# A hybrid convolution and RG-LRU block: recurrent channels laid out so that three of four heads fill the rows of one tile, and two low parts and a sum formed by accumulating DMA

## The chip, the cores and the metric

The kernel runs on one core of one Trainium2 chip. The metric is the device time of one execution in microseconds (us). Engines are named as the profile names them: PE (matrix multiply), PEld (its weight loads), DVE (vector), ACT (scalar, activations), POOL (GpSimd, used here to issue DMAs that add to their destination), SP (issues plain DMAs).

## The reference

One layer, sequence 1024, width 1024, everything in float32:

```python
h = rms_norm(x, g_mix)
z = h @ w_in + b_in                       # 1024 -> 7168
va, ga, xb, gb, sa, sb = split(z)         # 1024, 1024, 1536, 1536, 1024, 1024
u = causal_depthwise_conv(va * sigmoid(ga), conv_a_w, conv_a_b)      # width 31
y_a = silu(layer_norm(u)) @ w_a_out
v = causal_depthwise_conv(xb, conv_b_w, conv_b_b)                    # width 4
# rg_lru: 16 heads of 96 channels, block-diagonal 96x96 matrices
r = sigmoid(heads(v) @ w_rg_a + b_rg_a);  i = sigmoid(heads(v) @ w_rg_x + b_rg_x)
a = exp(-8 * r * softplus(-lam));         b = sqrt(1 - a*a) * i * v
h_t = a_t * h_{t-1} + b_t
y_b = (h * gelu(gb)) @ w_b_out
x = x + (sigmoid(sa) * y_a + sigmoid(sb) * y_b) @ w_o
x = x + square(relu(rms_norm(x, g_mlp) @ w_1)) @ w_2
out = rms_norm(x, g_final)
```

## The kernel before

Every float32 product is made of three products of rounded parts: a high part `h` and a low part `l = x - h` of each operand, and `hh + hl + lh` on PE. Low parts come either from `split` (ACT rounds, DVE subtracts) or from `split_dma`: ACT writes `l = -x` rounded, a POOL DMA adds `x` to it, ACT writes `h`. Channels stand on the 128 partitions, positions along the free axis (1024).

The change lies in the first projection stage and in what hangs on it. That stage is a hand-written order (`manual_schedule`: each engine executes its instructions in the order in which the Python code issues them). It goes through 28 column chunks of `w_in` of 128 columns each, in the order of the list `CH`. Chunks 0 to 2 are made earlier; **slot s** is the pass of the loop `for s in range(3, NC1)` in which PE makes chunk s (48 matmuls of 128x512; 24 pairs of operands, two halves) while the other engines work on the chunk before it. `CH` is XB0, VA0, GA0, XB1, XB2, VA1, GA1, XB3 to XB5, VA2, GA2, XB6 to XB8, VA3, GA3, XB9 to XB11, and then VA4, GA4 to VA7, GA7 in pairs. So the twelve `xb` tiles (12 x 128 = 1536 channels) come in four groups of three, and XB3, XB4, XB5 are taken out of the accumulator in slots 8, 9, 10.

What is done with an `xb` tile t: `xb_out` (ACT writes `xb` and a first tap of `v`, then three more taps of the width-4 convolution on DVE, called `rest` below), `xb_parts` (ACT writes the high half `vth`, DVE subtracts for the low half `vtl`). In the layout before, head n has channels 96n to 96n+95, which lie across tile borders: four heads fill three tiles. `head_load` therefore gathers a head's rows out of one or two tiles by SP DMAs (table `PIECES`). `head_mm(n, gi)` makes gate gi (0: r, 1: i) of a head, six matmuls into the one accumulator pair of tag `ps2`, which has a single buffer, so that PE cannot start a head product before ACT has read the one before. `head_gate` is that read: a sigmoid on ACT, and then SP DMAs scatter the 96 rows to one or two gate tiles `gate[gi, t]`.

Head n has slot `HS0[n]`: `head_mm(n, 0)` is at the end of that slot, `head_gate(n, 0)`, `head_mm(n, 1)` (after 36 of the 48 matmuls) and `head_gate(n, 1)` are in the next. In ACT's order within a slot stand `head_gate(before, 0)`, `xb_out`, the split of the next chunk's weights (`w_parts`: two copies), the square roots of `scan_root`, `xb_parts`, `head_gate(before, 1)`, the split of the next head's weights (`rgh`; DVE makes `rgl`), and the exponentials of `scan_exp`. Four heads are a group; `EXP` is the slot after the fourth head's: there ACT makes six exponentials and tanh, and `scan_in` (DVE: gate i times v) is issued for the group's first two tiles, and one slot later for its third. `scan_tile` is the recurrence itself. Slots of ten and more microseconds of DVE time that are not taken are filled by `fill` with taps of the width-31 convolution `conv` (one tap: one DVE instruction of 128x~511), whose count per slot a planner fixes at build time from assumed costs (`clk`); the order that comes of it is then fixed on the chip.

At the end of each of the eight convolutions its result `acc` goes to DRAM by SP, and DVE adds it to `ysum`, the sum that the layer norm later takes its mean from (128x1024).

## Time and profile before

| | |
|---|---|
| median of 3 runs | 1534.11 us (1533.87 to 1534.23) |
| the profiled execution | 1534.4 us, span 1532.6 us |
| granted PE clock | 0.999 |
| PE / PEld busy | 1522.9 us (99%) / 1252.9 us (82%) |
| DVE / ACT / POOL busy | 1217.2 us (79%) / 911.8 us (59%) / 172.6 us (11%) |
| instructions | 19039 |

The slots 3 to 27 lie between about 43 and 361 us of the span. A timeline row has the start in us, the duration in us, engine, line, operation, tiles and shape, a count, and in brackets the idle time before it with what ended it. A row of the chain has start, duration and what. Line numbers are those of the kernel before.

### The profile page before, as it was taken

Reading aid. Unit: us, or ns where it says so; the run is one execution under the profiler, and the core shown is the slowest. Engines: PE = TensorE matmul, PEld = TensorE weight load, DVE = VectorE, ACT = ScalarE, POOL = GpSimd, SP = SyncE. Lnnn points to the kernel's source line nnn. Section 1 sums busy time; section 2 is a strip of 40 time slices with the busy share of each in tenths; the row PEclk is TensorE's granted clock in tenths of the full one; section 3 lists DMA queues with packets and bytes.
Section 4 is the critical chain, followed back from the end, with each engine's and each line's share of the span. In section 5 each row is a group of like instructions: output and inputs, shape, how many; then the busy total and the mean of one; then the engine's idle time right before and its main releaser. Section 6 shows DMA issues by size and latency. Waiting matters only on the chain.

```text
span 1532.6 us, 19039 instructions
## 1 busy us (share of the span) xinstructions
PE 1522.9 (99%) x6734; PEld 1252.9 (82%) x6734; DVE 1217.2 (79%) x1647; ACT 911.8 (59%) x1273; POOL 172.6 (11%) x205
## 2 busy tenths in 40 slices
PE   9999999999999999999999999999999999999998
PEld 7878887888888888888888888888888888888886
DVE  6899999979999998778769879755555386777777
ACT  6648576657667666735475877554444455545475
POOL 0000000002222222000022322000000000101010
PEclk9999999999999999999999999999999999999999
DMA  8776978899998888963779898333333974776465
GB/s 349 198 188 159 250 185 215 223 274 224 241 255 209 198 193 229 311 230 117 265 199 301 197 194 210 138 117 112 112 112 110 304 266 124 177 209 170 109 123 153
DMA packets 132577, 304.68 MB, mean 199 GB/s; under 512 B 13264, under 2 KB 35280, under 8 KB 132480
## 3 DMA queue, kind: packets, MB, share of 16 engines
q1 hardware_dynamic: 104048, 234.79, 46.6%
q0 software_dynamic: 28288, 68.40, 24.4%
q8 instruction: 53, 0.87, 0.2%
q14 instruction: 44, 0.36, 0.1%
q10 hardware_dynamic: 144, 0.26, 0.0%
HBM read 149.79 MB, written 60.82 MB: 137 GB/s over the span
## 4 chain that ended last, share of the span: by engine, by line
PE 91%; issue 4%; DMA 2%; POOL 1%; DVE 1%; ACT 0%; SPq 0%; POOLq 0%; DVEq 0%
PE z L726 18%; PE d1b L1952 2%; PE d2b L1952 2%; PE d0b L1952 2%; PE d3b L1952 2%; PE d0e L1952 1%; PE d3e L1952 1%; PE d3a L1952 1%; PE d2e L1952 1%; PE d2a L1952 1%; PE d1e L1952 1%; PE d1a L1952 1%; PE z L258 1%; PE rg L534 1%; PE rg L536 1%
## 5 line engine op out<-in xcount | busy, mean ns | idle before, releaser
L726 PE MATMUL z<-xh,win_h 128*128 128x512 f32 x400 | 124.9, 390 | 0.0
L726 PE MATMUL z<-xl,win_h 128*128 128x512 f32 x400 | 124.5, 389 | 0.0
L726 PE MATMUL z<-xh,win_l 128*128 128x512 f32 x400 | 98.2, 391 | 0.0
L726 PEld LDWEIGHTS z<-xh,win_l 128*128 128x128 f32 x400 | 75.1, 188 | 16.9
L726 PEld LDWEIGHTS z<-xh,win_h 128*128 128x128 f32 x400 | 75.0, 188 | 16.7 <-ACT win_h L67 0.7
L637 DVE SCALAR_TENSOR_TENSOR y<-u,vec,y 128x511 f32<-128x511 f32 (+14 forms) x120 | 88.6, 739 | 0.0
L726 PEld LDWEIGHTS z<-xl,win_h 128*128 128x128 f32 x400 | 75.1, 188 | 15.8
L542 ACT ACTIVATE g<-rg,vec 96x1024 f32<-96x1024 f32 x32 | 35.6, 1113 | 85.4 <-issue 43.2
L637 DVE SCALAR_TENSOR_TENSOR yt<-u,vec,yt 128x511 f32<-128x511 f32 (+6 forms) x112 | 82.9, 740 | 0.0
L637 DVE SCALAR_TENSOR_TENSOR y<-yt,csum,y 128x511 f32<-128x511 f32 (+6 forms) x112 | 82.8, 739 | 0.0
L1648 ACT ACTIVATE o<-s 128x512 fp32r<-128x512 f32 x56 | 33.7, 623 | 45.7 <-DVE s L1632 26.4
L66 POOL DMA_DIRECT2D win_l<-win_raw x25 | 21.8, 871 | 325.0 <-ACT win_l L65 287.5
L486 DVE SCALAR_TENSOR_TENSOR v<-xb,vec,v 128x1023 f32<-128x1023 f32 (+2 forms) x36 | 46.2, 1283 | 6.9 <-ACT v L477 6.1
L66 POOL DMA_DIRECT2D zo<-zw x42 | 36.7, 874 | 127.7 <-ACT zo L65 114.6
L66 POOL DMA_DIRECT2D db_10l<-br x4 | 3.5, 874 | 339.3 <-DMA br<-in_w_dram 253.8
L1176 DVE TENSOR_TENSOR o<-s,o 128x512 fp32r<-128x512 f32 x56 | 37.3, 684 | 1.5 <-ACT o L1648 1.5
L65 ACT ACTIVATE zo<-zw 128x512 fp32r<-128x512 f32 x42 | 26.3, 625 | 20.1 <-PE z10f L914 2.1
L66 POOL DMA_DIRECT2D zo<-zs x28 | 24.5, 875 | 76.7 <-ACT zo L65 71.4
L578 DVE TENSOR_TENSOR_SCAN g<-a,g 128x1024 f32<-128x1024 f32 x12 | 27.5, 2292 | 0.4
L67 ACT ACTIVATE win_h<-win_raw 128x1024 fp32r<-128x1024 f32 x25 | 26.1, 1046 | 0.0
L65 ACT ACTIVATE win_l<-win_raw 128x1024 fp32r<-128x1024 f32 x25 | 26.1, 1045 | 0.0
L67 ACT ACTIVATE zo<-zw 128x512 fp32r<-128x512 f32 x42 | 26.1, 621 | 0.0
(3140 smaller groups left out, 4832.2 us busy)
## 6 DMA issues: line engine op xcount, KB each, us to landing
w_raw<-in_w_dram SPq DMA_DIRECT2D x34, 512.0 KB, 5.6
br<-in_w_dram SPq DMA_DIRECT2D x32, 512.0 KB, 5.9
ar<-fd SPq DMA_DIRECT2D x32, 512.0 KB, 6.8
zw<-in_w_in_dram SPq DMA_DIRECT2D x28, 512.0 KB, 5.7
win_raw<-in_w_in_dram SPq DMA_DIRECT2D x25, 512.0 KB, 7.4
win_l<-win_raw POOLq DMA_DIRECT2D x25, 512.0 KB, 7.3
zo<-zw POOLq DMA_DIRECT2D x42, 256.0 KB, 5.7
gates<-zg SPq DMA_DIRECT2D x32, 256.0 KB, 3.9
```

Source lines behind the costliest of these rows:

```text
L65: nc.scalar.activation(l, src, AF.Copy, scale=-1.0)
L66: nc.gpsimd.dma_start(l, src, accum_op=ALU.add)
L67: nc.scalar.activation(h, src, AF.Copy)
L258: nc.tensor.matmul(z0[i][:, HALVES[hf]], w0[i][w][:, k, :], xpart(a, hf, k), start=k == 0 and which == "hh", stop=k == 7 and which == ("hl ...
L486: nc.vector.scalar_tensor_tensor(v[:, d:S], a[:, 0:S - d], cbw_c[:, w * 12 + t:w * 12 + t + 1], v[:, d:S], ALU.mult, ALU.add)
L542: nc.scalar.activation(a, gps.pop((n, gi))[:HD, :], AF.Sigmoid, bias=(ba_c, bx_c)[gi][:, n:n + 1])
L578: nc.vector.tensor_tensor_scan(i, a, i, 0.0, ALU.mult, ALU.add)
L637: nc.vector.scalar_tensor_tensor(o[:, k:], a[:, 0:HS - k], c, o[:, k:], ALU.mult, add)
L726: nc.tensor.matmul(zps[s][:, HALVES[hf]], w[:, k, :], xw[k][part][hf], start=n == 0, stop=n == 23)
L1176: tt(l, src, h.bitcast(F32), ALU.subtract)
L1648: nc.scalar.activation(o[:, 0], src, AF.Copy)
L1952: nc.tensor.matmul(o, a, b, start=start and n == 0, stop=stop and n == len(todo) - 1, skip_group_check=not start or not stop)
```

## The change

- The recurrent channels (`xb`, `gb`, and with them their convolution weights, biases, `lam` and the rows of `w_b_out`) are permuted on the host. In each group of four heads, tile i (i = 0, 1, 2) holds head i in rows 0 to 95 and the i-th third (32 channels) of the fourth head in rows 96 to 127.
- Heads 0, 1 and 2 of a group are multiplied straight out of `vth`, `vtl`, and ACT writes their gates straight into the gate tiles. Only the fourth head is gathered (3 x 2 DMAs of 32 rows), and its two gates are scattered (3 x 2 DMAs of 32 rows).
- `xb_parts` uses `split_dma` in place of ACT + DVE.
- All heads are one slot earlier: `HS0` begins at 4, not 5, and `EXP` moves with it (8, 13, 18, 23 where it was 9, 14, 19, 24). The order of chunks is as it was.
- `head_load` is called at the head of a slot, for the tile of the slot before.
- `ysum` is written by a POOL DMA for the first convolution and accumulated by POOL DMAs for the other seven; a convolution has one planned step less (47 for 48).

```diff
-                taps["now"], taps["next"], taps["left"] = taps["next"], None, 48
+                taps["now"], taps["next"], taps["left"] = taps["next"], None, 47
...
-    PIECES = [[(0, 0, 96, 0)], [(0, 96, 128, 0), (1, 0, 64, 32)],
-              [(1, 64, 128, 0), (2, 0, 32, 64)], [(2, 32, 128, 0)]]
...
     def xb_parts(t):
         vp_[t] = T(f"vth{t}", F32R), T(f"vtl{t}", F32R)
-        nc.scalar.activation(vp_[t][0], vt[t], AF.Copy)
-        h = vp_[t][0].bitcast(F32)
-        later(at("A", 1.06), 1.22, nc.vector.tensor_tensor, vp_[t][1], vt[t], h, ALU.subtract)
+        split_dma(vt[t], *vp_[t])
+        at("A", 2.1)
...
-    def head_load(n):
-
-        g, hh = divmod(n, 4)
-        parts[n] = H(f"vh{n}", "p", F32R), H(f"vl{n}", "p", F32R)
-        for (ti, p0, p1, d0) in PIECES[hh]:
-            for a, b in zip(parts[n], vp_[3 * g + ti]):
-                nc.sync.dma_start(a[d0:d0 + p1 - p0, :].bitcast(F32), b[p0:p1, :].bitcast(F32))
+    def head_load(t):
+
+        n = 4 * (t // 3) + 3
+        if t % 3 == 0:
+            parts[n] = H(f"vh{n}", "p", F32R), H(f"vl{n}", "p", F32R)
+        for a, b in zip(parts[n], vp_[t]):
+            nc.sync.dma_start(a[32 * (t % 3):32 * (t % 3) + 32, :].bitcast(F32), b[HD:P, :].bitcast(F32))
+        parts[n - 3 + t % 3] = vp_.pop(t)
...
-        vh, vl = parts[n]
+        vh, vl = (a[:HD] for a in (parts.pop(n) if gi else parts[n]))
...
-        a = H(f"g{n}_{gi}", "g")
+        if hh < 3:
+            gate[gi, 3 * g + hh] = T(f"g{gi}_{3 * g + hh}")
+        a = gate[gi, 3 * g + hh][:HD] if hh < 3 else H(f"g{n}_{gi}", "g")
         nc.scalar.activation(a, gps.pop((n, gi))[:HD, :], AF.Sigmoid,
                              bias=(ba_c, bx_c)[gi][:, n:n + 1])
         at("A", 1.11, ready)
-        for (ti, p0, p1, d0) in PIECES[hh]:
-            t = 3 * g + ti
-            if (gi, t) not in gate:
-                gate[gi, t] = T(f"g{gi}_{t}")
-            nc.sync.dma_start(gate[gi, t][p0:p1, :], a[d0:d0 + p1 - p0, :])
+        if hh == 3:
+            for i in range(3):
+                nc.sync.dma_start(gate[gi, 3 * g + i][HD:P, :], a[32 * i:32 * i + 32, :])
...
         nc.sync.dma_start(yd[j], acc)
-        yield step()
         if j == 0:
             ysum.append(T("ysum"))
-            nc.vector.tensor_copy(ysum[0], acc)
+            nc.gpsimd.dma_start(ysum[0], acc)
         else:
-            nc.vector.tensor_tensor(ysum[0], ysum[0], acc, add)
-        yield step(1.22)
+            nc.gpsimd.dma_start(ysum[0], acc, accum_op=add)
+        yield step()
...
-    HS0 = [5 + 5 * (n // 4) + n % 4 for n in range(NH)]
+    HS0 = [4 + 5 * (n // 4) + n % 4 for n in range(NH)]
...
+    head_w(0)
     w_load(3)
...
             w_load(s + 2)
+            for t in sorted(vp_):
+                head_load(t)
...
-            if nxt is not None:
-                head_load(nxt)
...
+    r = np.arange(NH * HD).reshape(NH // 4, 4, HD)
+    rnn = np.concatenate([r[:, :3], r[:, 3].reshape(NH // 4, 3, 32)], 2).ravel()
...
-    wb = i["w_b_out"][0].reshape(12, P, 8, P)
+    wb = i["w_b_out"][0][rnn].reshape(12, P, 8, P)
...
-        "w_in": tiles(i["w_in"][0]),
+        "w_in": tiles(i["w_in"][0][:, z]),
```

More of the change, by code (lines that the diff above doesn't have):

```diff
@@ L2173, in layout @@
     mix = np.arange(D).reshape(2, 4, 4, 32).transpose(0, 2, 1, 3).ravel()
-    vecs = [cols(i[n][0]) for n in ("g_mix", "b_in")] + [cols(i["g_mlp"][0][mix])]
+    r = np.arange(NH * HD).reshape(NH // 4, 4, HD)
+    rnn = np.concatenate([r[:, :3], r[:, 3].reshape(NH // 4, 3, 32)], 2).ravel()
+    z = np.arange(7168)
+    for o in (2048, 3584):
+        z[o:o + NH * HD] = o + rnn
+    vecs = [cols(i["g_mix"][0]), cols(i["b_in"][0][z])] + [cols(i["g_mlp"][0][mix])]
     vecs += [cols(i[n][0]) for n in ("conv_a_b", "ln_g", "ln_b")]
-    vecs += [cols(i["conv_a_w"][0]), cols(i["conv_b_w"][0]), cols(i["conv_b_b"][0])]
-    vecs += [cols(i["lam"][0])] + [heads(i[n][0]) for n in ("b_rg_a", "b_rg_x")]
-    wb = i["w_b_out"][0].reshape(12, P, 8, P)
+    vecs += [cols(i["conv_a_w"][0]), cols(i["conv_b_w"][0][:, rnn]), cols(i["conv_b_b"][0][rnn])]
+    vecs += [cols(i["lam"][0][rnn])] + [heads(i[n][0]) for n in ("b_rg_a", "b_rg_x")]
+    wb = i["w_b_out"][0][rnn].reshape(12, P, 8, P)
     w2 = i["w_2"][0].reshape(DFF // 512, 2, 2, P, 2, HS).transpose(0, 2, 4, 3, 1, 5)
```

## The prediction

> **What bounds the kernel now.** I read the busy times first, then the chain that ended last, then who waits for whom on PE.

> ```profile
> PE 1522.9 (99%) x6734; PEld 1252.9 (82%) x6734; DVE 1217.2 (79%) x1647; ACT 911.8 (59%) x1273; POOL 172.6 (11%) x205
> PE 91%; issue 4%; DMA 2%; POOL 1%; DVE 1%; ACT 0%; SPq 0%; POOLq 0%; DVEq 0%
> PE spare L345 <- POOL ones L113: 1.6, 1, 1.6
> PE f1d L1660 <- DMA o<-s: 0.4, 1, 0.4
> PE d0b L1952 <- DVE da_61l L1176: 0.3, 1, 0.3
> ```

> PE is busy for 99% of the span, carries 91% of the chain, and has only three waits, 2.3 us in all. So work taken from DVE gives nothing back: nobody on the path waits for DVE. The change leaves PE's 6734 matmuls as they are, so the most it could gain is those 2.3 us, none of which lies in the slots that it touches. What it can do is make PE wait. The question is whether the new order brings each head's operands and its accumulator in time.

> **How a slot runs.** From the chain, slots 14 to 16 of the kernel before (start, duration, what):

> ```profile
> 184.50 8.18 PE z L726 x36
> 194.07 13.65 PE z L726 x60
> 209.11 8.18 PE z L726 x36
> 218.68 2.77 PE z L726 x12
> 222.84 7.27 PE z L726 x32
> ```

> A slot with two head products is 36 matmuls (8.18 us), a head product of 1.39 us to +9.57, 12 matmuls to +12.34 (218.68 + 2.77), a second head product to +13.73 (222.84 − 209.11). Slot 14 starts at 184.50; slot 16, two slots on, at 24.61 after it.

> Slot 14 holds the fourth head's second product, and its ACT order is the pattern that matters (in the changed kernel the same pattern starts in slots 8, 13 and 18; I call such a slot E and count from its start):

> ```profile
> 194.11 1.11 ACT L542 ACTIVATE g<-rg,vec 96x1024 f32<-96x1024 f32 x1 [0.39 <-PE rg L536]
> 203.49 1.10 ACT L474 ACTIVATE xb<-z,vec 128x1024 f32<-128x1024 f32 x1
> 204.62 1.25 ACT L477 ACTIVATE v<-xb,vec 128x1024 f32<-128x1024 f32 x1
> 205.77 1.04 ACT L65 ACTIVATE win_l<-win_raw 128x1024 fp32r<-128x1024 f32 x1
> 206.72 1.04 ACT L67 ACTIVATE win_h<-win_raw 128x1024 fp32r<-128x1024 f32 x1
> 209.07 2.96 ACT L566 ACTIVATE g<-g 128x1024 f32<-128x1024 f32 x3
> 211.94 1.04 ACT L494 ACTIVATE vth<-v 128x1024 fp32r<-128x1024 f32 x1
> 214.55 1.12 ACT L542 ACTIVATE g<-rg,vec 96x1024 f32<-96x1024 f32 x1
> ```

> After the sigmoid at +9.61 (released by PE) come the head's weight split, a table load and six exponentials, to +18.99; then `xb`, `v`, the weight split, roots, `vth`, and the next group's first sigmoid at +30.05, ending at +31.2. Slot E+2 has begun at 24.61, and PE wants that sigmoid done by 24.61 + 8.18 = 32.8: 1.6 us of slack. ACT is late here, and PE only just does not notice.

> **What is removed and costs or gains nothing.** DVE loses twelve `vtl` subtractions and the sums of the convolutions:

> ```profile
> 194.75 1.22 DVE L462 TENSOR_TENSOR vtl<-v,vth 128x1024 fp32r<-128x1024 f32 x1
> 185.00 1.22 DVE L651 TENSOR_TENSOR ysum<-ysum,y 128x1024 f32<-128x1024 f32 x1
> win_l<-win_raw POOLq DMA_DIRECT2D x25, 512.0 KB, 7.3
> DMA to landing us min/median/max: 4.5/7.3/10.3
> L66 POOL DMA_DIRECT2D zo<-zw x42 | 36.7, 874 | 127.7 <-ACT zo L65 114.6
> ```

> That is 12 × 1.22 + about 8 × 1.22, some 24 us of an engine that PE does not wait for; the planner fills the place with taps. POOL gets 20 DMAs of the `win_l` kind, 0.87 us each on POOL and 7.3 to landing (4.5 to 10.3). Behind them in POOL's queue stand the weight lows (`win_l`, later `zo`); POOL idles for ACT before most of those (114.6 us before this `zo` group alone), so I take 0. Were the four sums that fall among the `zo` loads fully on the path, 4 × 0.87 = 3.5 us. SP loses 48 DMAs, none of which PE waited for. Heads read in place cost PE the same 1.39 us.

> **What ACT gains.** Each of the twelve tiles costs one more copy, 0.95 us by the spacing of `win_l` and `win_h` above. In E the new copy hides in the wait for PE that ends at +9.61. In E+1 it lies on the late chain.

> **The two moves that cost.** First, the order of chunks is not moved while the heads are. Before, xb tiles are evacuated in E−1, E, E+1; now in E, E+1, E+2. In E+2 ACT must do, between the first head's two sigmoids: `xb` and `v` (2.3 us), wait for DVE's three taps, two copies. PE needs the second sigmoid by +12.34 of E+2, for the accumulator has one buffer. Second, all three gate tiles now hold rows of the fourth head. `scan_in` in E (the product of gate i with v for two tiles) formerly found its gates complete; now it must wait for the fourth head's second sigmoid and its scatter, and behind it in DVE's order stand taps, the next tile's `rest` and all that ACT makes of it.

> ```profile
> 188.65 3.92 DVE L486 SCALAR_TENSOR_TENSOR v<-xb,vec,v 128x1023 f32<-128x1023 f32 x3
> 192.48 2.36 DVE L462 TENSOR_TENSOR g<-g,v 128x1024 f32<-128x1024 f32 x2
> 195.88 0.35 DVE L462 TENSOR_TENSOR rgl<-rraw,rgh 96x192 fp32r<-96x192 f32 x1
> 196.15 0.74 DVE L637 SCALAR_TENSOR_TENSOR yt<-u,vec,yt 128x511 f32<-128x511 f32 x1
> 196.82 0.74 DVE L637 SCALAR_TENSOR_TENSOR y<-u,vec,y 128x510 f32<-128x510 f32 x1
> 205.90 1.28 DVE L486 SCALAR_TENSOR_TENSOR v<-xb,vec,v 128x1023 f32<-128x1023 f32 x1 [0.43 <-ACT v L477]
> g<-g SPq DMA_DIRECT2D x16, 128.0 KB, 5.1
> DMA to landing us min/median/max: 2.4/4.4/14.3
> ```

> In the row at 192.48 the products start with no idle time; a tap is 0.66 us from start to start. Now, from E's start, with the instructions counted in the order in which the changed kernel issues them: `rest` 3.5 to 7.4; second sigmoid 9.6 to 10.7; the 32-row scatter (128 KB) lands 5.1 later, at 15.8. The two products run to 18.2, one tap and `rgl` to 19.1, 14 taps (9.25) to 28.4, the next `rest` (3.85) to 32.2. Before, that `rest` began at +21.4, so it is now 7 us late. ACT: two copies 32.3 to 34.2, then as before 2.61 from `vth` to the sigmoid (211.94 to 214.55, the new copy ahead): 35.9 to 37.0. PE's second product, wanted at 32.8, waits 4.2. Then `xb` and `v` to 39.2, while DVE does a product, 7 taps, `rgl`, 4 taps (8.8) to 41.0 and the third `rest` to 44.85; two copies, sigmoid 46.8 to 47.9. PE wanted the next head product at 24.61 + 12.34 = 36.95 and starts it at 48.0. So a group costs 11.0 us, and DVE has caught up by the next E.

> In the first such group DVE is late as well:

> ```profile
> 118.58 8.18 PE z L726 x36
> 124.35 3.92 DVE L486 SCALAR_TENSOR_TENSOR v<-xb,vec,v 128x1023 f32<-128x1023 f32 x3
> ```

> Its `rest` starts at +5.8 (slot 14's at +4.15), 1.6 later; that pushes the sigmoid from 9.6 to about 10.9, so 12.3 for that group. Sum: 12.3 + 11.0 + 11.0 = 34.3.

> A fourth place: the last group's exponentials now stand in slot 23, before a chunk with its own sigmoid (`u`).

> ```profile
> 325.78 1.12 ACT L542 ACTIVATE g<-rg,vec 96x1024 f32<-96x1024 f32 x1 [5.57 <-issue]
> 334.91 1.04 ACT L65 ACTIVATE win_l<-win_raw 128x1024 fp32r<-128x1024 f32 x1
> 110.13 0.80 ACT L619 ACTIVATE y<-u,vec 128x512 f32<-128x512 f32 x1
> 110.83 0.71 ACT L620 ACTIVATE yt<-u,vec 128x512 f32<-128x512 f32 x1
> 213.25 1.28 ACT L542 ACT_TABLE_LOAD   x1
> ```

> From slot 23: sigmoid 9.6, 9.13 to the end of the exponentials (334.91 − 325.78), first taps 1.4, table 1.3, `u` 1.1 give 22.5, and two weight copies 24.5. PE begins slot 25 at 12.34 + 10.88 = 23.2: 1.3 us. The group of slots 4 to 7 has no exponentials ahead of it. Its tightest place is the first head:

> ```profile
> 55.23 1.06 ACT L494 ACTIVATE vth<-v 128x1024 fp32r<-128x1024 f32 x1 [1.35 <-DVE v L486]
> 53.93 22.06 PE z L726 x96
> ```

> The copy that starts the `vtl` DMA is done at 56.3, and the head product stands after slot 4's 48 matmuls, at 53.93 + 11.03 (half of 22.06) = 65.0: 8.7 us for a landing of 4.5 to 10.3. With that and the first head's second sigmoid behind tile 2 I estimate 0.5 (0 to 2).

> All: 34.3 + 1.3 + 0.5 = 36.1 us on the profiled execution's own 1534.4 (span 1532.6), 1570.5. The median shown is 0.3 lower, 1534.11, so 1570.

> [...] The scatter's 5.1 us is the row's. [...]

> **Rivals.**
> *The scatter is no brake (1551).* If the products of gate and v do not hold DVE up, only the moved evacuation stays: sigmoid at +31.0 (30.05 and one copy), ending 32.1, in time; `xb`, `v` to 34.4, `rest` to 38.3, copies and sigmoid to 41.4, 4.4 past 36.95. Three groups with the first at 5.8: 14.6, and 1.8 as above. It needs the products to stand later in DVE's order than I read it, or 7 us of taps to be missing behind them; DVE's 79% leaves such room over the whole span, and the order as counted speaks against it.
> *More than forecast (1579).* Each us by which the scatter lands later costs three. The `g` transfers took up to 14.3 us, and now they meet a `vtl` of 512 KB that ACT has released about a us before. At 8 us: 8.7 more.
> *Not slower (1534).* The place is PE's next head product in E+2, the price is everything above, and it decides if the sigmoid before it ends by +36.95. For it: the three waits of PE quoted first show that ACT has always kept this date so far, and DVE has 24 us less to do. Against it: that ACT work is 11 us late by my count and 4.4 even without the DVE wait, since `xb`, `v`, `rest` and two copies (8.2 us) now stand between the two sigmoids.

> **How the numbers follow.** A difference of about 0.2% (3 us) is what a measurement can tell from none. Forecast (1560 to 1577) 0.52; scatter no brake (1546 to 1560) 0.22; more than forecast 0.18; not slower 0.08, of which 0.02 faster by over 0.2% (PE has only 2.3 us to give) and 0.06 within. The range 1549 to 1581 leaves out the not-slower case, half of the upper case and a little of the lower one, 0.2 in all.

> **What would show it.** In the profile after: PE waits for ACT `g` in slots 10, 15 and 20, two per group (about 4 and 7 us); DVE waits for a scatter in slots 8, 13, 18 and 23; one wait of PE for `win_h` near slot 25; nothing past the first projection. It is wrong if PE shows no wait at its head products, if the waits are for `vtl` DMAs, or if the time is lost after slot 27.

## The result, and the profile after

The changed kernel takes 1582.67 us in the median (1581.7 to 1585.2, 4 runs) against 1534.17 (1533.87 to 1535.01) for the kernel before: a ratio of 1.0318, 95% interval 1.0300 to 1.0336, 48.5 us slower. The profiled execution took 1582.45 us, with a span of 1580.2 against 1532.6. It is the forecast's direction and, nearly place for place, the forecast's waits, but 12.7 us more than the 1570 and 1.7 us above the end of the range.

From the page of the kernel after: the busy times and the chain; then three lines of the view of PE's waits and one of DVE's (total us, number, longest).

```profile
PE 1537.9 (97%) x6734; PEld 1260.9 (80%) x6734; DVE 1194.4 (76%) x1627; ACT 924.2 (58%) x1286; POOL 189.4 (12%) x225
PE 76%; DVE 11%; issue 5%; DMA 4%; ACT 2%; POOL 1%; SPq 1%; POOLq 0%; DVEq 0%; ACTq 0%
PE rg L531 <- ACT g L541: 26.8, 6, 4.8
PE z0a L911 <- ACT z0b L949: 4.0, 1, 4.0
PE z L722 <- ACT win_h L67: 1.3, 1, 1.3
DVE g L462 <- DMA g<-g: 36.5, 4, 12.1
```

DVE has 23 us less to do, as meant, and yet it and a DMA now stand in the chain, where PE had 91%. DVE waits for the fourth head's scatter once in each of the four groups, as forecast. PE's waits grew from 2.3 us to some 35: six at head products, one at the weights of slot 25, one at the start of the second projection, and 3.1 us in four short ones that are not shown. And PE is busy for 15 us more with the same 6734 matmuls. That is the part that no wait shows. Stretches behind six of the waits, in the view by windows (stretch and length; busy us of PE, PEld, DVE, ACT, POOL; granted clock, DMA share, GB/s), and PE's matmuls there in the timeline:

```profile
144.10:147.60 3.50, 3.49 (x9) 2.54 (x10) 3.50 (x7) 3.47 (x4) 0.00 (x0) 0.58 0.59 119
222.60:226.30 3.70, 3.66 (x10) 2.66 (x11) 3.70 (x7) 3.67 (x4) 0.20 (x1) 0.58 0.41 82
233.30:236.90 3.60, 3.52 (x9) 2.51 (x10) 3.50 (x5) 0.89 (x3) 0.00 (x0) 0.53 0.94 236
312.10:318.50 6.40, 6.36 (x15) 4.74 (x16) 6.26 (x6) 3.24 (x4) 0.87 (x1) 0.50 0.96 247
368.80:372.30 3.50, 3.46 (x15) 2.87 (x16) 2.44 (x3) 3.49 (x4) 0.35 (x1) 1.00 0.88 167
411.60:417.60 6.00, 5.92 (x14) 4.68 (x15) 5.96 (x9) 4.31 (x7) 0.00 (x0) 0.50 0.49 119
233.92 0.63 PE L532 MATMUL rg<-vth,rgl 96*96 96x512 f32 x1
234.34 0.63 PE L533 MATMUL rg<-vtl,rgh 96*96 96x512 f32 x1
234.77 0.63 PE L531 MATMUL rg<-vth,rgh 96*96 96x512 f32 x1
```

Behind five of these six waits (3.65 to 4.98 us in the table below) PE runs at half clock: matmuls start 0.427 us apart, not 0.227, 8 of them in most places, 15 from 312.1 on, 14 from 411.6 on. The row at 368.80 is the one behind the short wait of 1.3 us: clock 1.00. On the page's 40 slices the clock reads 9 throughout; only narrow windows show it.

All the time added lies in the first 420 us. Counted from the starts of PE's matmuls, with 0.227 us as the normal spacing, in us (group 0 is the heads of slots 4 to 7; the waits of groups 1, 2 and 3 stand in slots 10, 15 and 20):

| place | wait | half clock behind it |
|---|---|---|
| group 1, first and second wait | 3.65, 4.95 | 1.59, 1.68 |
| group 2 | 4.49, 4.93 | 1.59, 1.67 |
| group 3 | 4.71, 4.98 | 1.59, 3.11 |
| weights of slot 25 | 1.46 | 0 |
| start of the second projection | 4.16 | 2.92 |
| sum | 33.3 | 14.15 |

Together 47.5, against 47.6 between the two spans.

The middle group (slots 13 to 15), PE, DVE and ACT from its timelines:

```profile
185.35 0.63 PE L722 MATMUL z<-xh,win_h 128*128 128x512 f32 x2
217.24 1.07 PE L722 MATMUL z<-xh,win_l 128*128 128x512 f32 x4
222.64 0.48 PE L531 MATMUL rg<-vth,rgh 96*96 96x512 f32 x1 [4.33 <-ACT g L541]
233.38 0.74 PE L531 MATMUL rg<-vth,rgh 96*96 96x512 f32 x1 [4.77 <-ACT g L541]
188.98 3.92 DVE L483 SCALAR_TENSOR_TENSOR v<-xb,vec,v 128x1023 f32<-128x1023 f32 x3 [1.85 <-ACT v L474]
201.47 2.36 DVE L462 TENSOR_TENSOR g<-g,v 128x1024 f32<-128x1024 f32 x2 [8.57 <-DMA g<-g]
213.90 3.91 DVE L483 SCALAR_TENSOR_TENSOR v<-xb,vec,v 128x1023 f32<-128x1023 f32 x3
226.32 3.91 DVE L483 SCALAR_TENSOR_TENSOR v<-xb,vec,v 128x1023 f32<-128x1023 f32 x3
195.12 1.11 ACT L541 ACTIVATE g<-rg,vec 96x1024 f32<-96x1024 f32 x1
217.90 1.06 ACT L65 ACTIVATE vtl<-v 128x1024 fp32r<-128x1024 f32 x1 [4.86 <-DVE v L483]
221.47 1.11 ACT L541 ACTIVATE g<-rg,vec 96x1024 f32<-96x1024 f32 x1
232.24 1.09 ACT L541 ACTIVATE g<-rg,vec 96x1024 f32<-96x1024 f32 x1
```

With E's start at 185.35, the forecast's own steps read:

| from E's start | forecast | measured |
|---|---|---|
| first `rest` begins | 3.5 | 3.6 |
| fourth head's second sigmoid | 9.6 | 9.8 |
| products of gate and v, after the scatter | 15.8 | 16.1 |
| next `rest` | 28.4 | 28.6 |
| the two copies | 32.3 | 32.6 |
| next group's first sigmoid | 35.9 | 36.1 |
| PE's first wait | 4.2 | 4.3 |
| third `rest` | 41.0 | 41.0 |
| second sigmoid | 46.8 | 46.9 |
| PE's second head product starts | 48.0 | 48.0 |

### The profile page after: what moved, and what is told of

Read it like the earlier page. It is cut to its first block, busy times and chain, and to the rows that moved or that the text cites. A ratio compares the mean times of both kernels' runs of the same rounds, so it can differ in the third digit from the quotient of the medians.

```text
span 1580.2 us, 18954 instructions
## 1 busy us (share of the span) xinstructions
PE 1537.9 (97%) x6734; PEld 1260.9 (80%) x6734; DVE 1194.4 (76%) x1627; ACT 924.2 (58%) x1286; POOL 189.4 (12%) x225
## 4 chain that ended last, share of the span: by engine, by line
PE 76%; DVE 11%; issue 5%; DMA 4%; ACT 2%; POOL 1%; SPq 1%; POOLq 0%; DVEq 0%; ACTq 0%
PE z L722 6%; DVE y L634 4%; DVE v L483 2%; PE d2b L1949 2%; PE d1b L1949 2%; PE d0b L1949 2%; PE z L258 2%; DVE yt L634 2%; PE d3b L1949 2%; PE d0e L1949 1%; PE d3e L1949 1%; PE d3a L1949 1%; PE d2e L1949 1%; PE d2a L1949 1%; PE d1e L1949 1%
## 5 line engine op out<-in xcount | busy, mean ns | idle before, releaser
L66 POOL DMA_DIRECT2D win_l<-win_raw x25 | 21.7, 868 | 260.8 <-ACT win_l L65 235.0
L66 POOL DMA_DIRECT2D zo<-zw x42 | 36.6, 871 | 131.0 <-ACT zo L65 129.2
L531 PE MATMUL rg<-vth,rgh 96*96 96x512 f32 x48 | 21.7, 453 | 26.8 <-ACT g L541 26.8
L65 ACT ACTIVATE zo<-zw 128x512 fp32r<-128x512 f32 x42 | 26.3, 627 | 32.6 <-DMA zw<-in_w_in_dram 10.3
L66 POOL DMA_DIRECT2D db_10l<-br x4 | 3.5, 873 | 339.7 <-DMA br<-in_w_dram 254.2
L462 DVE TENSOR_TENSOR g<-g,v 128x1024 f32<-128x1024 f32 x12 | 14.3, 1221 | 36.5 <-DMA g<-g 36.5
L65 ACT ACTIVATE vtl<-v 128x1024 fp32r<-128x1024 f32 x12 | 12.7, 1059 | 37.4 <-DVE v L483 30.3
L531 PEld LDWEIGHTS rg<-vth,rgh 96*96 96x96 f32 x48 | 8.6, 180 | 32.3 <-ACT g L541 29.6
L66 POOL DMA_DIRECT2D zo<-zs x28 | 24.4, 871 | 75.4 <-ACT zo L65 54.1
## 6 DMA issues: line engine op xcount, KB each, us to landing
w_raw<-in_w_dram SPq DMA_DIRECT2D x34, 512.0 KB, 5.4
br<-in_w_dram SPq DMA_DIRECT2D x32, 512.0 KB, 5.9
ar<-fd SPq DMA_DIRECT2D x32, 512.0 KB, 6.7
zw<-in_w_in_dram SPq DMA_DIRECT2D x28, 512.0 KB, 5.9
win_raw<-in_w_in_dram SPq DMA_DIRECT2D x25, 512.0 KB, 5.3
win_l<-win_raw POOLq DMA_DIRECT2D x25, 512.0 KB, 4.6
```

The source lines that it names most:

```text
L65: nc.scalar.activation(l, src, AF.Copy, scale=-1.0)
L66: nc.gpsimd.dma_start(l, src, accum_op=ALU.add)
L462: f(*a)
L531: nc.tensor.matmul(o, gh[:, gi, :], vh[:, hs], start=True, stop=False)
```

## The experiments

Theory A: two of the change's moves make the loss, each by itself. DVE's products of gate and v wait for the fourth head's scatter and hold up everything behind them; and the chunks are evacuated between a head's two sigmoids. What is measured beyond the waits is PE's clock. Rivals: the shift alone; a third cost in the accumulating DMAs or ACT's copies; slow matmuls from something other than PE's idle time.

| kernel | median us | ratio to before, 95% |
|---|---|---|
| `u_shift` | 1566.11 | 1.0198 (1.0181 to 1.0215) |
| `scan_later` | 1563.85 | 1.0185 (1.0169 to 1.0202) |
| `b_shift` | 1562.21 | 1.0166 (1.0140 to 1.0192) |
| `last_scan` | 1579.38 | 1.0290 (1.0274 to 1.0305) |
| `warm` | 1575.45 | 1.0270 (1.0253 to 1.0287) |
| `plan_gate_last` | 1545.58 | 1.0073 (1.0058 to 1.0088) |
| `u_plan` | 1535.80 | 1.0010 (1.0001 to 1.0020) |
| `u_plan_dve` | 1535.20 | 1.0007 (0.9998 to 1.0017) |

**u_shift: the shift undone.**

```diff
-    HS0 = [4 + 5 * (n // 4) + n % 4 for n in range(NH)]
+    HS0 = [5 + 5 * (n // 4) + n % 4 for n in range(NH)]
...
-    head_w(0)
```

> The changed kernel with its heads (and the slots of the exponentials that follow them) put back one slot, everything else of the change kept: layout, gates in place, accumulating DMAs. Theory A (two separate costs: DVE's product of gate and v waits for the fourth head's scatter, and the moved evacuations stand between two sigmoids): the second cost goes, the first stays. DVE still waits some 9 us for a scatter in each group, the rest of the tile behind it is late, PE waits once per group for the first head's first sigmoid, about 4.5 us with 1.7 us of half-clock matmuls behind it: 1534 + 3 x 6.2 = about 1553 (1546 to 1560), and no wait at the start of the second projection. Rival B (the shift alone makes the loss): 1534 to 1538, no PE wait over 1 us.

Measured 1566.11. PE's and DVE's waits, and a row of ACT's timeline:

```profile
PE rg L531 <- ACT g L541: 12.1, 3, 5.5
PE z L722 <- ACT win_h L67: 6.7, 1, 6.7
DVE g L462 <- DMA g<-g: 34.2, 4, 9.6
373.80 1.28 ACT L586 ACT_TABLE_LOAD   x1 [10.51 <-DVE g L575]
```

One wait per group is left, the first, as theory A has it, and DVE still waits for all four scatters. The shift alone (rival B) is out: without it 32 us of the loss stay. But the time is 13.1 us over 1553 and outside the expected range. In its profile 9.0 of the excess (6.9 of wait, 2.2 of half clock) stand at a place that I had not seen: in the last group DVE, late by its 9.6 us, still makes 23 planned steps of a convolution ahead of the first recurrence, ACT waits 10.51 us for that, and the next weights are 6.7 us late for PE. Most of the rest is half clock: 8.8 us behind the three head waits where I had 5.1.

**scan_later: the products one slot later.**

```diff
                     if d == 0:
                         scan_exp(g)
-                        scan_in(begun + 3.5, 3 * g, 3 * g + 1)
                     elif d == 1:
-                        scan_in(begun + 3.5, 3 * g + 2)
+                        scan_in(begun + 3.5, 3 * g, 3 * g + 1, 3 * g + 2)
```

> The changed kernel with the products of gate i and v of all three tiles issued one slot later (with the third tile's), nothing else changed. Theory A: DVE's waits for the scatter (36.5 us in four) go; the sigmoid before the first wait of each group is in time or 1.6 us late, the second wait stays at 4.4 us with a half-clock tail of 1.8 us: 3 x 6.2 + 1.6 + 1.5 = 21.7 us over the kernel before, 1556; if the wait at the start of the second projection (4.2 us and 3.1 us of half clock) stays, 1563. Rival B (the shift alone makes the loss, the scatter wait has cover): no change from 1582.7.

Measured 1563.85; the profiled execution had a span of 1558.6.

```profile
PE rg L531 <- ACT g L541: 14.1, 3, 5.0
PE z0a L910 <- ACT z0b L948: 2.7, 1, 2.7
PE z L722 <- ACT win_h L67: 1.3, 1, 1.3
```

The mirror image: the first wait of each group is gone and the second stays, 4.7 a group (I had 4.4), with 1.7 to 2.9 us of half clock behind each. DVE's wait for the scatter is gone from its list. So rival B's second half, that this wait has cover, falls too.

**b_shift: the shift alone, in the old layout.** The same line of `HS0` changed in the kernel before (5 to 4, and `head_w(0)` ahead of the loop).

> The kernel before with its heads moved one slot earlier, nothing else of the change (old layout with gathers, low halves and sums on DVE). Theory A: gates complete in time, so DVE does not wait for a scatter; only the evacuation between the first head's two sigmoids is new: the second sigmoid ends about 2.6 us late (one copy instead of two), too short for the half clock, and 1.5 us for the weights in slot 25: 1534 + 3 x 2.6 + 1.6 + 1.5 = 1545 (1538 to 1553). Rival B (the shift alone makes the loss): 1575 to 1583. Rival C (the old layout has the slack that the new one lost): 1534 to 1537.

Measured 1562.21, a miss of 17 us.

```profile
PE rg L534 <- ACT g L542: 10.0, 3, 4.0
PE z0a L915 <- ACT z0b L953: 2.0, 1, 2.0
PE z1a L915 <- DMA zo<-zw: 1.6, 1, 1.6
PE z0a L915 <- DMA zo<-zw: 1.5, 1, 1.5
```

The three waits are there, 10.0 us where I had 9.4. But the half clock came behind each of them, though one was only 2.8 us: 8.7 us in three. That 2.6 us is too short for it was my estimate, and no run had shown it: the kernel after has no wait between 1.6 and 3.6 us. And 11 us more are lost behind the start of slot 25, all but 1.6 of them at the start of the second projection. So the shift costs by itself about what the scatter wait costs by itself (u_shift): 28 and 32, but 48.5 together. In the groups the two do add. Counted from matmul starts, slot 25 begins 19.2 us late in `b_shift` and 21.2 in `u_shift`, and 40.5 in the kernel after, of which 1.5 are its wait for weights. What does not add is lost behind that point, at a different place in each: some 11, 9 and 7 us.

**last_scan: the last group's recurrences one slot later.**

```diff
-                    t = 3 * g + d - (2 if g < 3 else 1)
+                    t = 3 * g + d - 2
```

> The changed kernel with the last group's two recurrences one slot later (in slots 25 and 26 where the kernel before has them). Theory: the wait of 4.2 us at the start of the second projection, with its 3.1 us of half clock, comes of SP: the store of the recurrence's result stands ahead of eleven loads in SP's order and waits for a late DVE, so the loads of the second projection's weights are issued together and take 10 to 17 us. With the store behind them the wait goes: 7.3 us less, 1575.4. Rival: the loads are late because the memory traffic of that stretch is what it is, or ACT is late for another reason: within 1.5 us of 1582.7.

Measured 1579.38, 3.3 less, not 7.3. SP's waits between 350 and 390 us, the kernel after first, this one second:

```profile
SPq L576 <- DVE g L575: 13.6, 1, 13.6
```

```profile
SPq L60 <- DMA win_l<-win_raw: 11.0, 1, 11.0
```

The store no longer stops SP, but 11.0 of the 13.6 us come back at the next load, whose buffer is held by weights that ACT has split late. PE's wait at the second projection fell from 4.16 us to 2.37, and without half clock behind it. At that place the edit gains 4.6 us; the groups ahead of it, which it leaves alone, came out 1.1 later in this profile. So the store's order is a cause, but not of the whole loss there. The late split stands next in the chain; that it makes the 2.4 us left is not shown.

**warm: matmuls by zero where PE would wait.**

```diff
+    def fill_mm(s, n):
+        for _ in range(n if s - 2 in EXP and EXP[s - 2] < 3 else 0):
+            nc.tensor.matmul(zps[s][:, HALVES[0]], zero, xw[0][0][0], start=False, stop=False)
...
+                fill_mm(s, 14)
                 head_mm(before, 1)
             if s > 3:
-                chunk_mm(s, 18, 24)
+                chunk_mm(s, 18, 23)
+                fill_mm(s, 22)
+                chunk_mm(s, 23, 24)
```

> The changed kernel with matmuls by a zero matrix added (they add zero to the running chunk): 14 before the first wait and 22 before the second wait of each of the three groups, 3.2 and 5.0 us at 0.227, so that PE works in most of the time in which it would wait. Theory (idle time of PE over some 2.5 us halves its clock for the 8 to 15 matmuls behind): the slow matmuls behind the first waits go and the second wait takes their time (its end is ACT's), those behind the second waits go for good: 1.8 + 1.8 + 3.3 = 6.9 us less, 1575.8, granted clock near 1.00 at these places although PE does 108 matmuls more. Rival (the slow rows come of traffic or of what ACT and DVE do there): the slow rows stay, 1582.7 or more.

Measured 1575.45, with 108 matmuls more (`zero` is a 128x128 tile of zeros). The same stretch of clock as above, and that group's two waits with the matmuls by zero ahead of the second:

```profile
222.60:226.30 3.70, 3.70 (x18) 2.98 (x17) 3.70 (x7) 3.25 (x4) 0.87 (x1) 1.00 0.37 87
221.74 0.47 PE L533 MATMUL rg<-vth,rgh 96*96 96x512 f32 x1 [1.62 <-ACT g L543]
225.49 5.29 PE L730 MATMUL z<-xh,zero 128*128 128x512 f32 x22
232.50 0.47 PE L533 MATMUL rg<-vth,rgh 96*96 96x512 f32 x1 [1.25 <-ACT g L543]
```

18 matmuls in the stretch instead of 10, at clock 1.00, and no slow matmul behind any of the six places: the slow rows come of PE's idle time. The second head product still starts 10.76 us after the first (232.50 − 221.74; 233.38 − 222.64 = 10.74 in the kernel after), since ACT sets that date: the half clock behind the first wait had only eaten into the second. That the time agrees with the 1575.8 expected is in part luck. Up to the second projection the kernel gains 5.4 us, not 6.9; another 2.7 fall at the start of the second projection, which the edit does not touch (a wait of 2.7 and half clock of 1.7, for 4.2 and 2.9).

**u_plan: both moves taken back, the rest kept.** `HS0` as in u_shift, and

```diff
-                        scan_in(begun + 3.5, 3 * g, 3 * g + 1)
+                        scan_in(begun + 16.0, 3 * g, 3 * g + 1)
```

> The changed kernel with both suspected costs taken away: heads and exponentials back one slot, and the two products of gate i and v planned for 16 us (not 3.5) after the slot's start, so that DVE makes taps until the scatter has landed. Layout, gates in place and accumulating DMAs stay. Theory A (these two are all, with their half-clock tails): DVE no longer waits for g in each group, no PE wait over 2 us in slots 3 to 27, 1537 (1534 to 1542). Rival D (a third cost lies in the accumulating DMAs or in ACT's twelve extra copies): 1545 or more, with PE waits for a low half or for ACT.

**u_plan_dve: and the low halves and the sum on DVE.** As u_plan, with `xb_parts` and the two lines of `ysum` as in the kernel before.

> The kernel u_plan with the low halves of v and the sum of the convolutions made by DVE again: the new layout alone. Theory A: DVE is not on the path, so its 24 us more change nothing: within 2 us of u_plan. Rival D (the accumulating DMAs cost): faster than u_plan by over 3 us.

Measured 1535.80 and 1535.20: within 0.2% of the kernel before. PE's waits in u_plan, all of them, and DVE's for the scatter:

```profile
PE spare L345 <- POOL ones L113: 1.6, 1, 1.6
PE f1d L1656 <- DMA o<-s: 0.6, 1, 0.6
DVE g L462 <- DMA g<-g: 2.9, 2, 1.5
```

Theory A holds: the layout and the gates in place cost at most some 3 us (`u_plan` up to 1.0020), the accumulating DMAs nothing that this can measure (0.6 us apart, intervals overlapping), and none of them gains anything, as PE was already the bound. Rival D falls.

**plan_gate_last: the early heads kept, the order mended.** The line of u_plan for `scan_in`, the line of last_scan, and

```diff
+            if before is not None:
+                head_gate(before, 1, clk["P"] - 12 * MM)
             if s == 3 or c >= XB:
                 vector_work(0)
                 xb_parts(0 if s == 3 else c - XB)
-            if before is not None:
-                head_gate(before, 1, clk["P"] - 12 * MM)
```

> The changed kernel with its early heads kept and the order mended: the two products of gate and v planned 16 us after the slot's start, ACT's second sigmoid of a head put ahead of the copies of the v tile (so not behind DVE's taps), the last group's two recurrences one slot later. Theory A: both waits of each group are under 1 us, 1.5 us for the weights in slot 25 stay, the start of the second projection is under 3 us: 1540 (1535 to 1550). Rival: ACT has too much between the two sigmoids in any order, or the third tile's low half, now later, makes the third head wait: a wait of 3 to 5 us a group stays, 1555 or more.

Measured 1545.58.

```profile
PE z L722 <- ACT win_h L67: 4.4, 4, 1.9
PE rg L531 <- ACT g L541: 3.5, 6, 0.8
PE z0a L911 <- ACT z0b L949: 0.4, 1, 0.4
```

The six waits shrink from 26.8 us to 3.5 and none is followed by half clock. The wait at the start of the second projection is 0.4 us, where `last_scan` alone left 2.4; which of the other two edits does this was not separated. The weights now come late in four slots, 4.4 us. These three edits of order are worth 37 us, but no version beat the kernel before.

## Why the prediction was wrong

**Right: what bounds it, and the two moves.** PE had nothing to give, DVE's 24 us were worth nothing, and the waits are at the named products for the named reasons. The chain through E fits to 0.3 us at every step. Up to the start of the second head product the three groups cost 10.2, 11.0 and 11.3 us (32.5) against 12.3, 11.0 and 11.0 (34.3): only the lateness of the first was overdone. The weights of slot 25: 1.5 against 1.3. Group 0: nothing against 0.5. These terms make 34.0 where the text had 36.1. The POOL DMAs at zero and SP's at zero held too.

**Wrong: a wait was priced at its length.** The sum has no term for what PE does after it. Half clock behind the second wait of each group costs 1.7, 1.7 and 3.1, 6.5 in all; that behind the first wait (4.8) is free, because the second wait ends when ACT is ready, whatever PE does before. `warm` shows both: the second head product starts when it did, and 5.4 of the 6.5 us come back.

**Wrong: "nothing past the first projection".** 4.2 us of wait and 2.9 of half clock at the second projection's start, 7.1. The step that failed is the fourth place of the sum: it followed the last group's exponentials to the weights of slot 25 and stopped there, and of SP it priced only the DMAs that go. Moving `EXP` also moved the last group's recurrences, and their stores stand in SP's order ahead of the loads for the next stage; I had counted the exponentials of that slot and not the stores. The rows (DMA view from 381 to 385 us of the kernel after, then from 337 to 342 us of the kernel before):

```profile
zw<-in_w_in_dram SPq DMA_DIRECT2D x4, 512.0 KB, 16.2
hd<-g SPq DMA_DIRECT2D x1, 512.0 KB, 17.7
```

```profile
zw<-in_w_in_dram SPq DMA_DIRECT2D x4, 512.0 KB, 8.2
```

SP, stopped for 13.6 us, then issues its loads in one bunch, and the four `zw` loads take twice as long, 16.2 us in the median for 8.2. In the chain of the kernel after, a `zw` load of 17.2 us leads, by the copies of ACT behind it, to the `z0b` that PE waits for. The stores are not all of it: with them out of the way (`last_scan`) 2.4 of the 7.1 us stay. SP's next load is then held for 11.0 us by weights that ACT has split late; but `plan_gate_last` has the same hold, 12.9 us, and a wait of 0.4, so the cause of those 2.4 stays open. 36.1 − 2.1 + 6.5 + 7.1 = 47.6.

**The rivals.** "Not slower" fails: the sigmoid that had to end by +36.95 began at +46.9. "The scatter is no brake" fails: it is worth 18.8 us (scan_later). "More than forecast" is where the time fell, but not by its mechanism: that wanted 8 us for the scatter. The scatters of the fourth heads' second gates (views from 119 to 122, 195 to 199 and 274 to 277 us):

```profile
g<-g SPq DMA_DIRECT2D x3, 128.0 KB, 3.6
g<-g SPq DMA_DIRECT2D x3, 128.0 KB, 5.1
g<-g SPq DMA_DIRECT2D x3, 128.0 KB, 5.5
```

**The scatter's 5.1 us.** The middle row above, with a `vtl` transfer under way, has the 5.1 that the sum used. From 186 to 189 us, where only one other transfer was issued and the engines stood still before, the view has 2.3:

```profile
yd<-y SPq DMA_DIRECT2D x1, 512.0 KB, 3.0
g<-g SPq DMA_DIRECT2D x3, 128.0 KB, 2.3
```

So the same 128 KB took 2.3 to 5.5 us in the kernel after, and the 5.1 lies within that. What the sum lacked is the clock. By the numbers of the kernel after, an estimate of 8 matmuls at 0.2 us more (0.427 for 0.227) behind each of three second waits adds 4.8 to the 1570. Behind five of the six head waits the slow stretch is just that long (8 x 0.427 = 3.4 us); behind the other two waits of 4 us and more it is longer, 15 and 14 matmuls, 6.4 and 6.0 us.

## What to carry to other kernels

Price a wait of the bounding PE as its length plus a restart: in the kernel after 1.6 to 3.1 us behind every wait of 3.5 us or more, unless a later wait with its own date swallows it. When work moves by a slot, list every queue in which its DMAs now stand ahead of something else, SP's stores first; a planner's due time that ignores a DMA wait (3.5 us where the data land at 16) was enough here to stop DVE and what stood behind it in its order, for 36.5 us in four waits. And a layout that saves DMAs by letting one late producer complete all tiles trades transfers for a dependence: look for the first reader of each tile.
